# A GLA/GQA encoder on one core: weight negations ordered behind the weight casts, and the first norm sum in another part of a product

## The chip, the cores and the metric

The kernel runs on one core of a Trainium2 chip. It computes a two-layer encoder in a single launch. The metric is device time in microseconds (us). Each quoted time of a kernel is the median of several runs; the profile is one execution of its own, taken by the hardware profiler, and its time is given beside the median wherever both occur.

The core has five engines with a queue of instructions each: TensorE (PE in the profile, with its weight loads as PEld), VectorE (DVE), ScalarE (ACT), GpSimd (POOL) and SyncE (SP). Each queue is worked off in order, so an instruction that waits holds up everything behind it on its engine. Here SP does nothing but start loads from DRAM, and POOL does nothing but start accumulating transfers (a transfer whose destination is added to, not overwritten).

## The reference

The input is 512 tokens of width 1024, with 16 learned tokens put in front, so 528 columns. Each of the two layers is a feed-forward block, a mixer and another feed-forward block, all on normalised input and all added to the running state:

```python
D_MODEL, SEQ, DEPTH, N_META, D_FF = 1024, 512, 2, 16, 2816
def rmsnorm(x, g):
    return x * lax.rsqrt(jnp.mean(x * x, axis=-1, keepdims=True) + EPS) * g
def swiglu(x, w_gate, w_up, w_down):
    return (jax.nn.silu(x @ w_gate) * (x @ w_up)) @ w_down
for l in range(DEPTH):
    h = h + 0.5 * swiglu(rmsnorm(h, gain[l, 0]), w_gate[l, 0], w_up[l, 0], w_down[l, 0])
    h = h + mixer(rmsnorm(h, gain[l, 1]), ...)      # gated linear attention + grouped-query attention
    h = h + 0.5 * swiglu(rmsnorm(h, gain[l, 2]), w_gate[l, 1], w_up[l, 1], w_down[l, 1])
return rmsnorm(h, final_norm)[:, N_META:]
```

All inputs are float32. The change touches the four feed-forward blocks only.

## The kernel before

**Splitting.** Every float32 weight block of 128x1024 is split into a high and a low part: ScalarE casts it (`whi`, line 342), VectorE subtracts the cast from the block (`wlo`, line 343). Activations are split likewise. A product is then three sets of matmuls: high by high, high weight by low activation, low weight by high activation.

**Seven products in place of eight.** A feed-forward block is worked as 2x2 block products by a Strassen-like scheme with seven products. Gate and up weights go in 11 pairs (line 748), most of them by seven products of 24 matmuls each; the down product goes in 4 groups of seven products per block (function `seven`, line 867), 16 such groups in the kernel. In the steady stretch a unit consists of two pairs and one down group, 21 products. In tile names, `_00_8` means layer 0, first block, pair 8; numbers 11 to 14 stand for the four down groups, so `_00_13` is the third down group.

**Weight sums.** Five of the seven products use sums of the four blocks `w11`, `w12`, `w21`, `w22`. They are made like this: `base` loads `w21` into a sum buffer and an accumulating transfer adds `w22` to it (`base_sum`). `first_sums` (called once `w11` of the pair is on its way) makes two negated copies of `w11` on ScalarE (`negative`, line 290, names `s3` and `s2`), then has `w21` from DRAM added to `s3` and the base sum added to `s2` (`add`, line 295). `last_sum` makes a negated copy of `w12` (`s4`) and adds `s2` to it. The sums are then cast and split like any block: `whi<-s`.

**Buffers.** There are three buffers for raw blocks, four plus one each for the high and the low parts, and seven for sums. SP's loads wait for a free raw buffer, a cast waits until TensorE has done with the high part that its buffer held.

**What sets the order.** The program text is turned into queues by a scheduler that goes by priority and by dependencies: an instruction may stand ahead of others that precede it in the text when its inputs are held to be ready earlier. `with self.after(ins):` adds an order-only dependency: what stands inside comes behind `ins` on its queue. Before the change a negation has none, so the scheduler places it by its load.

**Other lines that the prediction speaks of.** The activations between gate/up and down: the partial products are copied out of PSUM (`c`, line 758) and added up on VectorE (line 763), scaled (788, 805), passed through silu on ScalarE (511), multiplied, and split into the high and low operands `g` of the down product by a cast on ScalarE (828) and a subtraction on VectorE (829). The blocks begin with pair products in another form (`first_pair`, line 703) that also needs the norm: squares, column sums by a matmul (540), `rs` (553, 511, 557), all from `norm.rs`, called inside `first_pair`.

Of the kernel before, what the change touches and what calls it, by code (L numbers as in the profile page):

```python
# [13 lines left out]
AF = mybir.ActivationFunctionType  # L14
# [58 lines left out]
def lasts(begin):  # L73
    return [2 * g + begin + 2 for g in range(SEVENS)]
# [132 lines left out]
class Groups:  # L207


    def __init__(self, tc):  # L210
        self.tc, self.layer, self.groups, self.counts = tc, 0, {}, {}
# [16 lines left out]
class Weights:  # L228
# [3 lines left out]
    def __init__(self, nc, after, raw, hi, lo, wts, win, wdn):  # L232
        self.nc, self.raw, self.hi_pool, self.lo_pool, self.wts, self.win, self.wdn = nc, raw, hi, lo, wts, win, wdn
        self.sum_pool = None
        self.loads = []
        for t, col in zip(PLAN, COLUMN):
            if t[0] == "op":
                self.loads.append(t[1:])
            elif col % SLAB == 0:
                self.loads.append(col // SLAB)  # L240
        self.at = {load: i for i, load in enumerate(self.loads)}
        self.made, self.fetched, self.got, self.summed, self.raws, self.second = 0, 0, {}, {}, {}, {}
        self.pos, self.behind, self.after = 0, None, after
        ops = [i for i, load in enumerate(self.loads) if not isinstance(load, int)]
        self.apart = set(ops[4::5])
        self.extra = None
        self.bases, self.agenda = [], []
        for i in ops:
            f, p, product = self.loads[i]
            if product == "1":  # L250
                early = p >= NPAIR or f == (0, 0) and p == 2 or p - 1 in lasts(f == (0, 0))
                at = i - LEAD * early
                self.bases.append((at, (f, p)))
                self.agenda += [(at, 0, (f, p))] + [(i, 1, (f, p))] * early
        self.bases.sort()
        self.agenda.sort()
# [30 lines left out]

    def negative(self, f, i, name, w):
        t = self.sum_pool.tile([P, SLAB], F32, tag="ws", name=f"{name}_{f[0]}{f[1]}_{i}")
        self.nc.scalar.activation(t, w, AF.Copy, scale=-1.0)  # L290
        return t

    def add(self, t, src):
# [33 lines left out]
    def make(self, upto):  # L327
        nc = self.nc
        while self.made < min(upto, len(self.loads)):
            self.fetch(self.made + 1)  # L330
            s = self.made
            load = self.loads[s]
            summed_first = not isinstance(load, int) and load[1] >= NPAIR and load[2] == "6"
            w = self.raws.pop(s, None)
            if w is None:
                w = self.summed.pop(load)
            hi = self.slab("whi", self.hi_pool, s in self.apart, f"whi{s}")
            lo = self.slab("wlo", self.lo_pool, s in self.apart, f"wlo{s}")
            for a in np.split(np.arange(SLAB), 2 if s == 0 else 1):
                cs = slice(a[0], a[-1] + 1)  # L340
                with self.after(self.behind if load == ((0, 0), 2, "6") or load in RESERVED or summed_first else None):
                    nc.scalar.copy(hi[:, cs], w[:, cs])  # L342
                nc.vector.tensor_tensor(lo[:, cs], w[:, cs], hi[:, cs].bitcast(F32), ALU.subtract)  # L343
            self.got[s] = (hi, lo)
            self.got.pop(s - 12, None)
            self.made += 1
            if not isinstance(load, int):
                if load[2] == "1" and load[:2] not in self.second:
                    self.first_sums(*load[:2], w)
                elif load[2] == "2":  # L350
                    self.last_sum(*load[:2], w)
# [39 lines left out]
def build(tc, ctx, xt, wts, win, wdn, par, w2, const, umask, out):  # L391
    nc = tc.nc
# [12 lines left out]
    def after(ins):  # L405
        return tc.issue_after(ins) if ins is not None else nullcontext()
# [36 lines left out]
    def pair(second=False):  # L443
        return (slots["s2"] if second else pss).tile([P, 2, 512], F32, tag="s2" if second else "ss", name=nm("ss"))
# [227 lines left out]
    def ffn(l, f, norm, done, following):  # L672

        x, rs, n = norm.x, None, live[0]
        w = n // 2
# [13 lines left out]
        def quarters():  # L689
            return slots["c"].tile([P, 4 * T], F32, tag="c", name=nm("c"))[:, : 4 * n].rearrange("p (j q c) -> p j q c", j=2, q=4)  # L690
# [3 lines left out]
        def first_pair(p, m):  # L694

            accs = [pair(m == "1") for _ in range(2)]
            blocks = [W.op((l, f), p, m + c) for c in "12"]
            for r, (hi, lo) in enumerate(blocks):
                for k, (first, second) in enumerate(zip(x, norm.second)):
                    for j, acc in enumerate(accs):  # L700
                        for i, (a, b) in enumerate(((hi, 0), (hi, 1), (lo, 0))):
                            for t, v in enumerate((first, second)):
                                last = TE.matmul(acc[:, t, :w], a[:, j, k], v[b][:, r], start=k == 0 and r == 0 and i == 0,  # L703
                                                 stop=k == len(x) - 1 and r == 1 and i == 2)
                    if (p, m, r, k) == (1, "2", 1, 0):
                        with after(last.ins):
                            factor.append(norm.rs("s2", urgent=False))
            st = made.setdefault(p, {})
            if "c" not in st:
                st["c"] = quarters()  # L710
            at = 2 * (m == "2")
            for j, acc in enumerate(accs):
                with tc.high_priority():
                    W.behind = S.copy(st["c"][:, j, at : at + 2], acc[:, :, :w]).ins
# [179 lines left out]
        for i, step in enumerate(steps):  # L894
            now[0] = i
            if step[0] == "P":
                product_of_pair(*step[1:])
                if step[2] == "7" and rs is None:
                    rs = norm.rs("ss" if second(step[1]) else "s2", urgent=False)
                if i == last_op:  # L900
                    close_pools(norm.pools)
                    following()
            elif step[0] == "F":
                for c in SQUARES.get(step[1:], ()):
                    norm.square(c)
                first_pair(*step[1:])
                if step[1:] == (1, "1"):
                    for j in range(KC // 2):
                        norm.pair(j)
                elif step[1]:  # L910
                    rs = factor.pop()
                    for m in range(2):
                        hidden(made[0], 0, m)
                        put_off(i + 1, lambda m=m: hidden(made[1], 1, m))
            elif step[0] == "O":
                two_products(*step[1:])
            elif step[0] == "S":
                seven(*step[1:])
            else:
                down(*step[1:])  # L920
            for fn in later.pop(i, ()):
                fn()
# [635 lines left out]
```

## Time and profile before

| | |
|---|---|
| median of three runs | 2216.25 us (2212.53 to 2220.52) |
| the profiled execution | 2211.28 us |
| its span, first to last instruction | 2209.5 us |
| TensorE busy with matmuls / weight loads | 2158.2 us (98%) / 2072.5 us (94%) |
| VectorE busy | 1719.5 us (78%) |
| ScalarE busy | 1378.2 us (62%) |
| GpSimd busy (issuing transfers) | 204.1 us (9%) |
| negations: 174 on ScalarE | 183.6 us |
| weight casts from blocks, sums and raw slabs: 241 + 174 + 126 | 252.6 + 182.8 + 132.3 us |

Profile rows name a group of instructions by line, engine, operation and tiles (`out<-in`, numbers left out), how often it occurs, its busy time, the mean duration of one in ns, and the idle time of the engine just ahead of it with what ended that idle time. Timeline rows give start and duration in us from the start of the span. The busy share of TensorE is from modelled ends of pipelined matmuls, so a wait of a few tenths of a microsecond can be hidden in it; the idle time ahead of weight loads shows more of them.

### The profile page before, as it was taken

Reading aid. Unit: us, or ns where it says so; the run is one execution under the profiler, and the core shown is the slowest. Engines: PE = TensorE matmul, PEld = TensorE weight load, DVE = VectorE, ACT = ScalarE, POOL = GpSimd, SP = SyncE. Lnnn points to the kernel's source line nnn. Section 1 sums busy time; section 2 is a strip of 40 time slices with the busy share of each in tenths; the row PEclk is TensorE's granted clock in tenths of the full one; section 3 lists DMA queues with packets and bytes.
Section 4 is the critical chain, followed back from the end, with each engine's and each line's share of the span. In section 5 each row is a group of like instructions: output and inputs, shape, how many; then the busy total and the mean of one; then the engine's idle time right before and its main releaser. Section 6 shows DMA issues by size and latency. Waiting matters only on the chain.

```text
span 2209.5 us, 40509 instructions
## 1 busy us (share of the span) xinstructions
PE 2158.2 (98%) x16572; PEld 2072.5 (94%) x16572; DVE 1719.5 (78%) x2627; ACT 1378.2 (62%) x2022; POOL 204.1 (9%) x236
## 2 busy tenths in 40 slices
PE   9999999999999999999999999999999999999998
PEld 9899999999999999999999999999888888999997
DVE  7888877577976688888688888775789867878885
ACT  8666646355784576666586666554567937666654
POOL 1111100000000011111011111000000001111100
PEclk9999999999999999999999999999999999999999
DMA  8788843211113688888488888532221238878851
GB/s 249 174 200 210 204 112 125 80 60 64 39 39 108 155 196 204 207 193 198 128 194 209 193 198 202 128 125 77 67 69 47 70 103 205 190 192 206 205 152 64
DMA packets 90746, 322.60 MB, mean 146 GB/s; under 512 B 10048, under 2 KB 12352, under 8 KB 90560
## 3 DMA queue, kind: packets, MB, share of 16 engines
q0 software_dynamic: 33408, 121.65, 30.5%
q1 hardware_dynamic: 55072, 195.13, 26.5%
q10 hardware_dynamic: 2080, 3.23, 0.4%
q8 instruction: 130, 2.13, 0.4%
q14 instruction: 56, 0.46, 0.1%
HBM read 257.06 MB, written 2.10 MB: 117 GB/s over the span
## 4 chain that ended last, share of the span: by engine, by line
PE 77%; DVE 9%; ACT 7%; DMA 5%; issue 2%; DVEq 0%; ACTq 0%; SPq 0%
PE ss L748 29%; PE ss L867 14%; PE mm L528 12%; PE ss L528 10%; DMA w<-win 5%; DVE wlo L343 3%; ACT whi L342 3%; PE ss L703 2%; PE sm L528 2%; PE sm L1237 1%; PE ss L1211 1%; ACT t L511 1%; ACT s L290 1%; PE sm L1255 1%; PE sm L1256 1%
## 5 line engine op out<-in xcount | busy, mean ns | idle before, releaser
L748 PE MATMUL ss<-xc,whi 128*128 128x264 f32 (+1 forms) x4608 | 841.6, 284 | 4.7 <-ACT c L758 4.7
L748 PEld LDWEIGHTS ss<-xc,whi 128*128 128x128 f32 x4608 | 714.6, 189 | 6.1 <-ACT c L758 5.9
L748 PE MATMUL ss<-xc,wlo 128*128 128x264 f32 (+1 forms) x2304 | 653.9, 284 | 0.0
L748 PEld LDWEIGHTS ss<-xc,wlo 128*128 128x128 f32 x2304 | 434.5, 189 | 0.0
L528 PE MATMUL mm<-x,whi 128*128 128x264 f32 (+1 forms) x1712 | 383.2, 314 | 0.0
L342 ACT CAST whi<-w 128x1024 fp32r<-128x1024 f32 (+1 forms) x241 | 252.6, 1048 | 179.3 <-PE ss L748 151.9
L867 PE MATMUL ss<-g,whi 128*128 128x264 f32 (+1 forms) x1792 | 336.5, 287 | 25.6 <-DVE g L829 13.1
L343 DVE TENSOR_TENSOR wlo<-w,whi 128x1024 fp32r<-128x1024 f32 (+1 forms) x241 | 293.5, 1218 | 84.5 <-ACT whi L342 84.1
L867 PEld LDWEIGHTS ss<-g,whi 128*128 128x128 f32 x1792 | 280.6, 190 | 31.6 <-DVE g L829 16.4
L528 PEld LDWEIGHTS mm<-x,whi 128*128 128x128 f32 x1712 | 278.3, 188 | 15.7 <-DVE x L517 0.2
L343 DVE TENSOR_TENSOR wlo<-s,whi 128x1024 fp32r<-128x1024 f32 x174 | 212.6, 1222 | 99.9 <-ACT whi L342 99.6
L342 ACT CAST whi<-s 128x1024 fp32r<-128x1024 f32 x174 | 182.8, 1051 | 131.6 <-PE ss L748 64.5
L528 PE MATMUL mm<-x,wlo 128*128 128x264 f32 (+1 forms) x856 | 264.5, 314 | 0.0
L867 PE MATMUL ss<-g,wlo 128*128 128x264 f32 (+1 forms) x896 | 255.1, 285 | 0.0
L290 ACT ACTIVATE s<-w 128x1024 f32<-128x1024 f32 x174 | 183.6, 1057 | 73.2 <-DMA w<-win 41.7
L342 ACT CAST whi<-raw 128x1024 fp32r<-128x1024 f32 x126 | 132.3, 1050 | 144.9 <-PE mm L528 69.1
L343 DVE TENSOR_TENSOR wlo<-raw,whi 128x1024 fp32r<-128x1024 f32 x126 | 154.0, 1222 | 78.8 <-ACT whi L342 78.0
L867 PEld LDWEIGHTS ss<-g,wlo 128*128 128x128 f32 x896 | 170.6, 190 | 0.0
L528 PEld LDWEIGHTS mm<-x,wlo 128*128 128x128 f32 x856 | 159.6, 188 | 7.4
L871 DVE TENSOR_TENSOR h<-h,ss 128x528 f32<-128x528 f32 (+1 forms) x224 | 154.2, 697 | 8.7 <-PE ss L867 5.3
L528 PE MATMUL ss<-g,whi 128*128 128x264 f32 (+1 forms) x764 | 142.7, 302 | 1.3 <-ACT g L516 1.3
L528 PEld LDWEIGHTS ss<-g,whi 128*128 128x128 f32 x764 | 111.6, 188 | 6.9 <-ACT g L516 1.5
(300 smaller groups left out, 3342.5 us busy)
## 6 DMA issues: line engine op xcount, KB each, us to landing
w<-win SPq DMA_DIRECT2D x175, 512.0 KB, 4.6
raw<-wts SPq DMA_DIRECT2D x126, 512.0 KB, 3.4
w<-wdn SPq DMA_DIRECT2D x64, 512.0 KB, 5.1
s<-w POOLq DMA_DIRECT2D x58, 512.0 KB, 6.2
s<-s POOLq DMA_DIRECT2D x58, 512.0 KB, 5.8
w<-win POOLq DMA_DIRECT2D x42, 512.0 KB, 8.6
s<-win POOLq DMA_DIRECT2D x42, 512.0 KB, 7.8
w<-wdn POOLq DMA_DIRECT2D x16, 512.0 KB, 7.6
```

Of the source, the lines that this page charges most:

```text
L290: self.nc.scalar.activation(t, w, AF.Copy, scale=-1.0)
L342: nc.scalar.copy(hi[:, cs], w[:, cs])
L343: nc.vector.tensor_tensor(lo[:, cs], w[:, cs], hi[:, cs].bitcast(F32), ALU.subtract)
L511: prev_act[0] = S.activation(*args, **kw).ins
L528: TE.matmul(acc.half[i][:width], lhs, rhs[:, acc.spans[i]], start=first, stop=last)
L703: last = TE.matmul(acc[:, t, :w], a[:, j, k], v[b][:, r], start=k == 0 and r == 0 and i == 0, stop=k == len(x) - 1 and r == 1 and i == 2)
L748: TE.matmul(acc[:, j], a[:, j, k], b[:, at], start=bool(begin and k == 0 and i == 0), stop=k == len(x) - 1 and i == 2, skip_group_check=no ...
L867: TE.matmul(acc[:, j], a[:, 2 * half + j, k], b, start=bool(begin and k == 0 and i == 0), stop=k == 1 and i == 2, skip_group_check=not begin)
L871: V.tensor_tensor(to, to, acc, ALU.add)
L1211: TE.matmul(s[:n, i, :HF], lhs, kh[:, hs], start=True, stop=False)
L1237: TE.transpose(tp[:, j * w + u * n : j * w + (u + 1) * n], pr[:n, (2 * c2 + j) * P : (2 * c2 + j + 1) * P], ident[:n, :n])
L1255: TE.matmul(o[:, :w], vw, ph, start=i == 0, stop=False)
```

## The change

Two things change. First, the weight cast keeps its instruction in `self.latest`, and `negative` is issued with an order-only dependency on it: each negation stands on ScalarE's queue behind the weight cast that precedes it in the text. Second, in the first block only, the column sums of the norm (`norm.rs`) are called after the step (row 0, chunk 1) of a product of pair 1 in place of (row 1, chunk 0). No arithmetic is added or left out.

```diff
@@ class Weights, __init__
-        self.extra = None
+        self.extra = self.latest = None
@@ negative
         t = self.sum_pool.tile([P, SLAB], F32, tag="ws", name=f"{name}_{f[0]}{f[1]}_{i}")
-        self.nc.scalar.activation(t, w, AF.Copy, scale=-1.0)
+        with self.after(self.latest):
+            self.nc.scalar.activation(t, w, AF.Copy, scale=-1.0)
         return t
@@ make
                 with self.after(self.behind if load == ((0, 0), 2, "6") or load in RESERVED or summed_first else None):
-                    nc.scalar.copy(hi[:, cs], w[:, cs])
+                    self.latest = nc.scalar.copy(hi[:, cs], w[:, cs]).ins
                 nc.vector.tensor_tensor(lo[:, cs], w[:, cs], hi[:, cs].bitcast(F32), ALU.subtract)
@@ first_pair
-                    if (p, m, r, k) == (1, "2", 1, 0):
+                    if (p, m, r, k) == (1, "2", 0, 1):
                         with after(last.ins):
                             factor.append(norm.rs("s2", urgent=False))
```

After the change, line numbers from 291 on are one higher (342 becomes 343, and so on). Queues before and after are quoted below by row; a row has the line, the operation and the tiles with their numbers.

ScalarE's queue where the third down group of the first block begins (`c119` is the gate/up activation of that group, `g132` to `g137` its split operands, `whi65` the cast of the sum `s2` of group 13, `s3_00_8` and `s2_00_8` the negations for pair 8), before:

```order
L342 CAST whi64_2611<-s4_00_7_2350 128x1024
L511 ACTIVATE c119_2256<-c119_2256 128x528
L290 ACTIVATE s3_00_8_2783<-w11_00_8_2756 128x1024
L342 CAST whi65_2646<-s2_00_13_2505 128x1024
L828 CAST g132_2604<-c119_2256 128x528
L290 ACTIVATE s2_00_8_2785<-w11_00_8_2756 128x1024
L758 COPY c130_2438<-ss129_2407 128x2x264
L828 CAST g135_2641<-c119_2256 128x528
```

The same place with the change:

```order
L343 CAST whi64_2611<-s4_00_7_2350 128x1024
L512 ACTIVATE c119_2256<-c119_2256 128x528
L343 CAST whi65_2646<-s2_00_13_2505 128x1024
L829 CAST g132_2604<-c119_2256 128x528
L343 CAST whi66_2683<-w12_00_13_2615 128x1024
L759 COPY c130_2438<-ss129_2407 128x2x264
L829 CAST g135_2641<-c119_2256 128x528
L291 ACTIVATE s4_00_13_2687<-w12_00_13_2615 128x1024
L343 CAST whi67_2721<-s3_00_13_2503 128x1024
L829 CAST g137_2676<-c119_2256 128x528
L845 ACTIVATE g139_2680<-c119_2256 128x264
L343 CAST whi68_2752<-w21_00_13_2412 128x1024
```

The two negations of pair 8 no longer stand between the silu and `g135`; they follow behind `whi68`. The negation `s4` of group 13, which stood in front of `whi61`, now follows `g135`.

ScalarE's queue a little earlier, where the negated copy `s2` of group 13 is made (the sum that `whi65` casts), with the change:

```order
L759 COPY c119_2256<-ss118_2226 128x2x264
L291 ACTIVATE s3_00_13_2503<-w11_00_13_2476 128x1024
L291 ACTIVATE s2_00_13_2505<-w11_00_13_2476 128x1024
L343 CAST whi61_2509<-s3_00_7_2268 128x1024
L343 CAST whi62_2543<-w11_00_13_2476 128x1024
```

Before, `s2_00_13` stood two casts further up, in front of `whi59`, and `s3_00_13` one cast above that; both now stand directly in front of `whi61`, one behind the other, and GpSimd starts their transfers in the same order as before.

ScalarE's queue in the first block, around the copy `c63` of the first product of pair 3, before:

```order
L342 CAST whi13_839<-s3_00_2_341 128x1024
L516 CAST t58_776<-c21_319 128x528
L511 ACTIVATE c34_576<-c34_576 128x528
L342 CAST whi14_875<-w12_00_3_798 128x1024
L516 CAST t60_783<-c21_319 128x528
L511 ACTIVATE c34_576<-c34_576 128x528
L290 ACTIVATE s3_00_11_1039<-w11_00_11_1012 128x1024
L758 COPY c63_824<-ss62_787 128x2x264
```

With the change:

```order
L343 CAST whi12_788<-w11_00_3_651 128x1024
L715 COPY c34_576<-ss52_644 128x528
L517 CAST t60_783<-c21_319 128x528
L291 ACTIVATE s3_00_3_792<-w11_00_3_651 128x1024
L291 ACTIVATE s2_00_3_794<-w11_00_3_651 128x1024
L759 COPY c63_824<-ss62_787 128x2x264
L512 ACTIVATE c34_576<-c34_576 128x528 x2
L343 CAST whi13_839<-s3_00_2_341 128x1024
```

The copy `c63` now comes before `whi13`; it stood behind `whi13`, `whi14`, the silus and the negation `s3` of group 11. In their place the two negations of pair 3 stand in front of it. The norm's chain (553, 511, 557), which stood between `whi11` and `whi12`, stands between `whi10` and `whi11` with the change.

## The prediction

> **What bounds the kernel now.** I read the page's busy times and chain first, then the waits of TensorE, then the timelines of the engines around one such wait.
>
> ```profile
> PE 2158.2 (98%) x16572; PEld 2072.5 (94%) x16572; DVE 1719.5 (78%) x2627; ACT 1378.2 (62%) x2022; POOL 204.1 (9%) x236
> PE 77%; DVE 9%; ACT 7%; DMA 5%; issue 2%; DVEq 0%; ACTq 0%; SPq 0%
> ```
>
> ```profile
> 300.00:420.00 120.00, 120.00 (x986) 119.71 (x985) 73.21 (x96) 54.70 (x74) 0.00 (x0) 1.00 0.31 99
> ```
>
> TensorE is the bound by sheer work, and where it has its operands (the 120 us from 300 to 420, the second row) it is busy without a gap at granted clock 1.00. So the number of matmuls sets a floor that the change does not touch, and only gaps of TensorE can be won or added. Yet 23% of the chain is not TensorE: each such piece is a place where it had to wait. The waits tell where.
>
> ```profile
> PE ss L867 <- DVE g L829: 13.1, 16, 0.8
> PE ss L867 <- ACT g L828: 12.5, 10, 3.2
> PE ss L748 <- ACT c L758: 4.7, 5, 3.0
> ```
>
> ```profile
> L867 PEld LDWEIGHTS ss<-g,whi 128*128 128x128 f32 x1792 | 280.6, 190 | 31.6 <-DVE g L829 16.4 <-ACT g L828 15.2
> ```
>
> The first two rows are one event each time: the start of a down group, waiting for its first operands `g`, the high part from ScalarE and the low part from VectorE. There are 16 down groups and 16 waits of the second kind, none above 0.8 us; 10 of the groups have the ScalarE wait on top. By the matmuls' modelled ends that is 25.6 us; by the weight loads (last row), which carry no modelled end, 31.6 us, or 1.98 us a group. I take 31.6.
>
> One of the 16, the third group of the first block, on TensorE, ScalarE, VectorE:
>
> ```profile
> 221.57 0.51 PE L867 MATMUL ss<-g,whi 128*128 128x264 f32 x2 [0.31 <-ACT g L828]
> 222.91 0.39 PE L867 MATMUL ss<-g,whi 128*128 128x264 f32 x1 [0.84 <-DVE g L829]
> ```
>
> ```profile
> 214.57 1.05 ACT L342 CAST whi<-s 128x1024 fp32r<-128x1024 f32 x1 [1.37 <-PE ss L748]
> 216.72 0.65 ACT L511 ACTIVATE c<-c 128x528 f32<-128x528 f32 x1 [1.10 <-DVE c L788]
> 218.99 1.06 ACT L290 ACTIVATE s<-w 128x1024 f32<-128x1024 f32 x1 [1.62 <-DMA w<-win]
> 219.95 1.03 ACT L342 CAST whi<-s 128x1024 fp32r<-128x1024 f32 x1
> 220.89 0.63 ACT L828 CAST g<-c 128x528 fp32r<-128x528 f32 x1
> ```
>
> ```profile
> 218.48 0.71 DVE L834 TENSOR_TENSOR c<-c 128x528 f32<-128x528 f32 x1
> 221.01 1.23 DVE L343 TENSOR_TENSOR wlo<-s,whi 128x1024 fp32r<-128x1024 f32 x1 [1.36 <-ACT whi L342]
> 222.16 0.70 DVE L829 TENSOR_TENSOR g<-c,g 128x528 fp32r<-128x528 f32 x1
> ```
>
> ```profile
> 213.98 4.92 DMA w<-win
> ```
>
> ScalarE is free at 217.37, after the silu. Next in its queue stands a negation for pair 8, work for a product still far off, and its `w11` was only issued at 213.98 and lands at 218.90 (last row, from the chain of waits). So ScalarE stands 1.62 us, negates for 1.06, casts `whi65`, and only then the high operand `g132` that TensorE wants; VectorE has `wlo65` ahead of the low operand in its queue, so the delay passes on to it. This is the wait behind a load, summed over the kernel:
>
> ```profile
> ACT s L290 <- DMA w<-win: 41.7, 18, 5.7
> ```
>
> **The change, part by part.**
>
> *1. Negations behind the casts (the main term).* The queue now runs silu, `whi65`, `g132`. When could `whi65` start? It needs a buffer that TensorE gives back once per product; `whi64` got its one at 214.57, a product takes 24 matmuls of about 0.122 us, 2.92 us, so 217.49. Then `whi65` ends near 218.5, `g132` runs to about 219.1. TensorE would reach that operand, without the 0.31 us, at about 221.1: on time by two. On VectorE `wlo65` can start at 219.2, when the L834 instruction ends, takes 1.23, then `g133` ends at about 221.1; TensorE wants it two matmuls after the high part, 221.3. So both waits fit, the second with only 0.2 us over. I keep 0.2 us a group, 3.2 in all (0 to 0.5 a group are the bounds: VectorE may have one more short instruction of 0.43 in front). Term: -31.6 + 3.2 = **-28.4**.
>
> *2. The sums come later.* The negation of group 13's `s2` stood here:
>
> ```profile
> 199.38 1.06 ACT L290 ACTIVATE s<-w 128x1024 f32<-128x1024 f32 x1 [1.29 <-DVE wlo L343]
> 203.84 0.59 ACT L758 COPY c<-ss 128x528 f32<-128x528 f32 x1
> ```
>
> ```profile
> 200.84 0.88 POOL L295 DMA_DIRECT2D s<-w  x1 [6.35 <-ACT s L290]
> 207.75 0.87 POOL L295 DMA_DIRECT2D s<-s  x1 [6.03 <-DMA s<-w]
> ```
>
> Its transfer was issued on GpSimd at 200.84. Now `s3` and `s2` both follow the copy at 203.84: 204.4 to 206.5, and the transfers start at about 205.5 and 206.6. The second must have landed at 217.5 to leave `whi65` where part 1 puts it: 10.9 us. What these transfers took:
>
> ```profile
> s<-w POOLq DMA_DIRECT2D x1, 512.0 KB, 6.3
> ```
>
> ```profile
> 761.22 1.24 POOL L295 DMA_DIRECT2D s<-win  x1
> 763.28 0.87 POOL L295 DMA_DIRECT2D s<-w  x1 [0.82 <-ACT t L601]
> ```
>
> ```profile
> s<-win POOLq DMA_DIRECT2D x1, 512.0 KB, 10.7
> s<-w POOLq DMA_DIRECT2D x1, 512.0 KB, 12.4
> ```
>
> ```profile
> s<-w POOLq DMA_DIRECT2D x58, 512.0 KB, 6.2
> ```
>
> The first is this one, 6.3 us between 200 and 214; the next are a pair issued 2 us apart, at 761.22 and 763.28, and each took about twice as long. The last row is the median of all 58. Now they go out a microsecond apart in all groups, so the price lies between 6.2 (0 late) and 12.4 (1.5 late). I take 8 to 10, no delay, since SP's loads here are few; with 12.4 it would cost up to 1.5 us a group, and since `whi65` stood at 219.95 before, even that leaves something of the gain. The base of pair 8 (`w21`) is now loaded behind its `w11` and its addition stands on GpSimd behind `s4` of group 13, whose negation now comes at about 225 (the transfer started at 207.75 before).
>
> ```profile
> 233.81 1.05 ACT L342 CAST whi<-w 128x1024 fp32r<-128x1024 f32 x1 [0.38 <-PE ss L867]
> 242.62 1.06 ACT L342 CAST whi<-s 128x1024 fp32r<-128x1024 f32 x1 [0.93 <-PE ss L867]
> ```
>
> These are the casts of `w11` and `s2` of pair 8. The sum lands near 241 for a cast at 242.62: tight, but a cast is made some four products, 11 us, before TensorE uses it, so a late sum there delays only the short copies behind it. For such new waits I add **+1.5**, bounds 0 and 9 (the 42 gate/up sums, each a fifth of a microsecond).
>
> Raw blocks: `w11` is held until its negations are done, now a little after its own cast; 2 x 1.06 us later, with SP's next load not due for several microseconds. Nothing on ScalarE is added: 174 negations stay 174.
>
> *3. The norm in the first block.*
>
> ```profile
> 52.62 0.65 ACT L557 ACTIVATE t<-rs 128x528 f32<-128x528 f32 x1
> 53.81 1.06 ACT L342 CAST whi<-w 128x1024 fp32r<-128x1024 f32 x1
> ...
> 62.73 0.64 ACT L511 ACTIVATE c<-c 128x528 f32<-128x528 f32 x1
> 64.38 1.06 ACT L290 ACTIVATE s<-w 128x1024 f32<-128x1024 f32 x1 [1.01 <-ACT c L511]
> 65.34 0.58 ACT L758 COPY c<-ss 128x528 f32<-128x528 f32 x1
> ```
>
> ```profile
> 62.62 0.40 PE L748 MATMUL ss<-xc,whi 128*128 128x264 f32 x2
> 65.98 0.81 PE L748 MATMUL ss<-xc,whi 128*128 128x264 f32 x2 [2.96 <-ACT c L758]
> ```
>
> TensorE stands 2.96 us until the copy `c63` has emptied the PSUM tile that the next product adds to. That copy waits behind the silus, which need `rs`, and a negation. With the change `rs`, whose last step on ScalarE is the row at 52.62, is there some 4.4 us sooner (the call is three steps earlier in its product, each 12 matmuls of 0.122 us), and the copy stands ahead of the silus, behind the two negations of pair 3, which can be over at about 59: `whi12` was cast at 53.81, and a copy, a cast of 0.64 and two negations follow it, 4 us with gaps of a few tenths. Without the wait TensorE would want it at about 63, when the matmul before it starts. I keep 0.5: **-2.5** (bounds -2.96 and 0).
>
> *4. Other copies.* The remaining 1.7 us of that row (4.7 in 5 waits, less 2.96) are four copies at the beginnings of the other blocks, each behind a negation. Some of these negations move away: **-0.9** (bounds -1.7 and 0).
>
> Sum: -28.4 + 1.5 - 2.5 - 0.9 = **-30.3**. The profiled execution took 2211.28 us (span 2209.5), which gives 2181.0; it lies 5 us below the median of the three runs, 2216.25, and just below their lowest. On the median it is **2186**, which I predict.
>
> **The rivals.**
>
> *A. The sums are late, and the kernel gets slower.* One mechanism: transfers in pairs land so late that `whi65` waits for `s2` at the head of ScalarE's queue, with `g132` behind it. It decides once `whi65` would start after 219.95, that is, from a landing time of 219.95 - 206.6 = 13.3 us. For it: the 12.4 us pair, one microsecond short; 1.13 us more between the two issues there than here. Against: the median of 6.2. Each microsecond beyond costs 16 us; at 15.5 us, +2.2 x 16 = +35, so 2251. The Trainium skill ("DMA: Bandwidth & Descriptors", section "Issuing engines are not separate DMA queues") says that transfers from all issuing engines run on the same 16 DMA engines and interleave, which speaks for a collision with SP's loads. The trace agrees in the 10.7 and 12.4 us rows; by that rule alone 12.4 would be the figure, and the gain up to 24 us smaller.
>
> *B. VectorE takes over.* `g132` is early but the low operand stays behind `wlo65` and other VectorE work, or the sums are late within the bound. Then the 13.1 us of waits for L829 stay, and of 31.6 only 15.2 to 18.5 go. With -2.5 and -0.9 and some +3 for late sums: -15 to -18, about 2200. For it: every one of the 16 groups shows that wait, whatever ScalarE did, and my margin is 0.2 us. Against: in the rows above VectorE idles 1.36 us for `whi65` just before.
>
> *C. The wait is one of buffers and only moves.* The load of `w11` was issued at 213.98 because a raw block came free then; if late blocks set the pace, a cast instead of a negation will wait for it. Then nothing is won: within 3 us of 2216, so 2213 to 2216. Against: the block of pair 8 is cast 14 us later than it landed, at 233.81. The Trainium skill ("Perfetto Trace Analysis", "Identifying Performance Opportunities") says that the same bubble repeated on the saturated engine can mean that memory for the next tile ran out. The bubble repeats 16 times here, but the rows show ScalarE free and an operand's source ready, so the trace bears this out little.
>
> *D. Only the first block gains*, if ScalarE's order in the 16 groups were not what was in the way: -2.5, 2213.
>
> **How the numbers follow.** The forecast has 0.62, B 0.20, C and D together 0.11, A 0.07. The forecast's own range is 2174 (36.3 us, all waits of parts 1, 3 and 4, go, and the base is about 2211) to 2197 (residual of 0.5 a group, 8 us, and 9 us for sums). The range that should hold the time 8 times in 10 reaches over B: 2173 to 2207. A measurement of this kernel can tell about 0.3%, 6.6 us, from no change. Forecast and B lie below 2209.6: faster 0.82. C and D are within: same 0.11. A: slower 0.07.
>
> **What would show it.** In the profile of the changed kernel: the L867 rows of TensorE's waits shrink from 25.6 us to under 4 and the weight-load row from 31.6 to under 6 (1); the row for negations waiting for `w<-win` shrinks from 41.7 to a few microseconds, and the chain no longer passes from that load to L290 (1); no long wait of a cast for a sum (`whi` for the transfer `s<-w`) in front of `g` (2, A); the wait at 65.98 under 1 us (3). If the ScalarE wait is gone and the VectorE wait of about 0.8 stays in 16 groups, B was right; if casts wait for `w<-win` by as much, C. The forecast is wrong if the span is above 2198 or below 2172.

## The result

| | before | with the change |
|---|---|---|
| median | 2215.03 us (2212.53 to 2220.52) | **2181.90 us** (2179.88 to 2182.74) |
| span of the profiled execution | 2209.5 us | 2180.6 us |
| idle ahead of the down groups' weight loads (867 / 868) | 31.6 us | 0.0 us |
| idle ahead of the gate/up products' weight loads (748 / 749) | 6.1 us | 14.6 us |
| casts waiting for a sum's transfer `s<-w` | none listed | 102.8 us, 29 times |

The change makes the kernel faster: the ratio is 0.9846, with a 95% interval of 0.9825 to 0.9866, 33 us at the medians (28.9 us between the two profiled spans). The forecast was 2186 and its range 2173 to 2207.

The page of the changed kernel, busy times and chain:

```profile
PE 2148.4 (99%) x16572; PEld 2067.0 (95%) x16572; DVE 1712.3 (79%) x2627; ACT 1369.9 (63%) x2022; POOL 204.1 (9%) x236
...
PE 81%; DVE 6%; ACT 5%; DMA 4%; issue 3%; POOL 0%; SPq 0%; DVEq 0%; ACTq 0%; POOLq 0%
PE ss L749 32%; PE ss L868 14%; PE mm L529 14%; PE ss L529 11%; DMA s<-w 3%; PE sm L529 2%; DVE wlo L344 1%; DMA w<-win 1%; ACT whi L343 1%; PE sm L1238 1%; PE ss L1212 1%; ACT t L512 1%; PE sm L1256 1%; PE sm L1257 1%; PE ss L1213 1%
```

TensorE's share of the chain rises from 77% to 81%. The loads of weights from DRAM (`w<-win`) fall in the chain from 5% to 1%, and L290/291, the negation, is no longer listed; a new entry is the sums' transfer, `DMA s<-w`, at 3%.

Two groups before, the weight loads of the gate/up products and the casts of sums:

```profile
L748 PEld LDWEIGHTS ss<-xc,whi 128*128 128x128 f32 x4608 | 714.6, 189 | 6.1 <-ACT c L758 5.9
L342 ACT CAST whi<-s 128x1024 fp32r<-128x1024 f32 x174 | 182.8, 1051 | 131.6 <-PE ss L748 64.5 <-PE ss L867 59.8 <-issue 4.2
```

With the change, the groups of weight loads, of casts of sums and of negations:

```profile
L749 PEld LDWEIGHTS ss<-xc,whi 128*128 128x128 f32 x4608 | 713.9, 189 | 14.6 <-ACT c L759 11.3 <-DVE c L764 3.0
L868 PEld LDWEIGHTS ss<-g,whi 128*128 128x128 f32 x1792 | 277.0, 188 | 0.0
L343 ACT CAST whi<-s 128x1024 fp32r<-128x1024 f32 x174 | 180.9, 1047 | 182.5 <-DMA s<-w 102.8 <-PE ss L749 43.9 <-PE ss L868 28.5
L291 ACT ACTIVATE s<-w 128x1024 f32<-128x1024 f32 x174 | 179.9, 1055 | 9.7 <-DMA s<-s 9.7
```

The second row is the main term, gone altogether. The last row: negations waited 41.7 us for `w<-win`; now none do. The first and third rows show what came in exchange. The same down group as in the prediction, on ScalarE, VectorE and TensorE:

```profile
211.99 0.65 ACT L512 ACTIVATE c<-c 128x528 f32<-128x528 f32 x1 [1.05 <-DVE c L789]
212.81 1.05 ACT L343 CAST whi<-s 128x1024 fp32r<-128x1024 f32 x1 [0.17 <-PE ss L749]
213.77 0.63 ACT L829 CAST g<-c 128x528 fp32r<-128x528 f32 x1
```

```profile
214.37 1.22 DVE L344 TENSOR_TENSOR wlo<-s,whi 128x1024 fp32r<-128x1024 f32 x1
215.51 0.70 DVE L830 TENSOR_TENSOR g<-c,g 128x528 fp32r<-128x528 f32 x1
```

```profile
216.36 0.41 PE L868 MATMUL ss<-g,whi 128*128 128x264 f32 x2
216.60 0.28 PE L868 MATMUL ss<-g,wlo 128*128 128x264 f32 x1
```

The cast `whi65` follows the silu by 0.17 us, the high operand is there at 214.40, two microseconds ahead of the matmuls at 216.36 that want it. The low operand ends at 216.21, one or two tenths of a microsecond ahead of its use. The cover on VectorE is as thin as reckoned, but in this kernel it holds in all 16 groups; with the negations alone (first experiment) one group waits 0.7 us there.

### The profile page after: what moved, and what is told of

Read it like the earlier page. It is cut to its first block, busy times and chain, and to the rows that moved or that the text cites. A ratio compares the mean times of both kernels' runs of the same rounds, so it can differ in the third digit from the quotient of the medians.

```text
span 2180.6 us, 40542 instructions
## 1 busy us (share of the span) xinstructions
PE 2148.4 (99%) x16572; PEld 2067.0 (95%) x16572; DVE 1712.3 (79%) x2627; ACT 1369.9 (63%) x2022; POOL 204.1 (9%) x236
## 4 chain that ended last, share of the span: by engine, by line
PE 81%; DVE 6%; ACT 5%; DMA 4%; issue 3%; POOL 0%; SPq 0%; DVEq 0%; ACTq 0%; POOLq 0%
PE ss L749 32%; PE ss L868 14%; PE mm L529 14%; PE ss L529 11%; DMA s<-w 3%; PE sm L529 2%; DVE wlo L344 1%; DMA w<-win 1%; ACT whi L343 1%; PE sm L1238 1%; PE ss L1212 1%; ACT t L512 1%; PE sm L1256 1%; PE sm L1257 1%; PE ss L1213 1%
## 5 line engine op out<-in xcount | busy, mean ns | idle before, releaser
L749 PEld LDWEIGHTS ss<-xc,whi 128*128 128x128 f32 x4608 | 713.9, 189 | 14.6 <-ACT c L759 11.3
L868 PE MATMUL ss<-g,whi 128*128 128x264 f32 (+1 forms) x1792 | 327.0, 283 | 0.0
L343 ACT CAST whi<-s 128x1024 fp32r<-128x1024 f32 x174 | 180.9, 1047 | 182.5 <-DMA s<-w 102.8
L868 PEld LDWEIGHTS ss<-g,whi 128*128 128x128 f32 x1792 | 277.0, 188 | 0.0
L868 PE MATMUL ss<-g,wlo 128*128 128x264 f32 (+1 forms) x896 | 253.9, 283 | 0.0
L868 PEld LDWEIGHTS ss<-g,wlo 128*128 128x128 f32 x896 | 168.7, 188 | 0.0
L529 PE MATMUL ss<-g,whi 128*128 128x264 f32 (+1 forms) x764 | 142.8, 302 | 1.3 <-ACT g L517 1.3
```

The costliest lines, as they stand in the source:

```text
L343: self.latest = nc.scalar.copy(hi[:, cs], w[:, cs]).ins
L529: TE.matmul(acc.half[i][:width], lhs, rhs[:, acc.spans[i]], start=first, stop=last)
L749: TE.matmul(acc[:, j], a[:, j, k], b[:, at], start=bool(begin and k == 0 and i == 0), stop=k == len(x) - 1 and i == 2, skip_group_check=no ...
L868: TE.matmul(acc[:, j], a[:, 2 * half + j, k], b, start=bool(begin and k == 0 and i == 0), stop=k == 1 and i == 2, skip_group_check=not begin)
```

## The experiments

All kernels below ran beside the kernel before on the same chip; ratios are to it.

**1. The two parts apart.** One kernel has only the ordered negations (the `r, k` test put back to `1, 0`), the other only the norm's move.

> The change without its second part: negations behind the casts, the norm's column sums where they were. Theory (the gain is the 16 down groups' wait): L868 rows of TensorE's waits stay at 0, the first block's wait for the copy c63 comes back in part (0 to 3 us, with up to 1.2 us of slow matmuls behind it), so 0 to 4 us above the full change, 2182 to 2186. Rival (the norm's move does a third or more of it, since it starts the first block earlier and shifts all that follows): 2192 or more.

> The change without its first part: only the norm's column sums move. Theory: the 31.6 us ahead of L867's weight loads stay as they are; the wait of 2.96 us at 66 us and the slow matmuls behind it (1.2 us) go, a new wait at the column sums (1.6 us in the full change at 45.8) comes: 1 to 4 us below before, 2211 to 2214. Rival (the norm's move does a third or more): 2204 or less.

Negations alone: 2180.41 us (2179.16 to 2181.41), ratio 0.9847 (0.9830 to 0.9864), a little below what its theory had. Norm alone: 2214.17 us, ratio 0.9995 (0.9981 to 1.0009). The whole gain is in the negations; the norm's move gives nothing that can be measured, a little less than its theory had. Why shows in the waits of TensorE with the norm's move alone, and in the row at its column sums:

```profile
PE ss L540 <- ACT t L534: 3.6, 1, 3.6
```

```profile
49.25 0.81 PE L540 MATMUL ss<-t,whole 128*128 128x264 f32 x2 [3.58 <-ACT t L534]
```

The wait of 2.96 us at 65.98 is gone, but not because its copy comes sooner: the first copy of line 758 starts at 66.99 here, against 65.34 before. TensorE comes there later, because the column sums, put earlier into the product, now wait 3.58 us for their operand. In the kernel with the negations alone there is no wait at 66 us either, and there the copy does come sooner: it starts at 61.35, ahead of the two casts and the negation behind which it stood before (two other negations, of pair 3, now precede it). A wait of 1.4 us for a copy comes at 75.7 us instead.

**2. The late sums.** What is left, 14.6 us ahead of the gate/up products, was put down to sums. At the beginning of the last block, with the change, on ScalarE and TensorE:

```profile
1866.77 1.05 ACT L343 CAST whi<-s 128x1024 fp32r<-128x1024 f32 x1 [5.55 <-DMA s<-w]
1867.72 0.63 ACT L512 ACTIVATE c<-c 128x512 f32<-128x512 f32 x1
1868.26 1.03 ACT L343 CAST whi<-s 128x1024 fp32r<-128x1024 f32 x1
1869.71 0.62 ACT L829 CAST g<-c 128x512 fp32r<-128x512 f32 x1 [0.43 <-DVE c L806]
1870.24 1.04 ACT L343 CAST whi<-w 128x1024 fp32r<-128x1024 f32 x1
1871.18 0.58 ACT L759 COPY c<-ss 128x512 f32<-128x512 f32 x1
```

```profile
1871.82 0.51 PE L749 MATMUL ss<-xc,whi 128*128 128x256 f32 x2 [2.77 <-ACT c L759]
```

A cast stands 5.55 us for the transfer of its `s2`; a silu, two more casts and the copy (759) pile up behind it; the matmul that wants the PSUM tile emptied by that copy waits 2.77 us. If that is the cause, the sums concerned must come earlier. They are those of pairs whose `first_sums` is called right after their own cast of `w11`; with the change their negations stand behind that cast. The next kernel leaves these alone free:

```diff
-    def first_sums(self, f, i, w):
-        s3, s2 = [self.negative(f, i, n, w) for n in ("s3", "s2")]
+    def first_sums(self, f, i, w, ordered=True):
+        s3, s2 = [self.negative(f, i, n, w, ordered) for n in ("s3", "s2")]
@@ negative
-        with self.after(self.latest):
+        with self.after(self.latest if ordered else None):
@@ make
-                    self.first_sums(*load[:2], w)
+                    self.first_sums(*load[:2], w, ordered=False)
```

> The full change, but the negations s3 and s2 of the pairs whose sums are formed only after their own cast of w11 are free again (as before the change); those of the pairs and groups formed ahead of it, and all s4, stay ordered. Theory (the 14.6 us that are left ahead of L749's weight loads come from casts that stand at the head of ScalarE's queue for a late sum): casts' wait for the transfer s<-w falls from 102.8 us to under 35, the L749 wait from 14.6 to under 5, L868 stays at 0: 2170 to 2175. Rival one (those waits come from where the copies now stand, not from the sums): within 2 us of 2182. Rival two (freed negations return to the place in front of g): L868 waits come back, 2190 or more.

2172.65 us (2170.78 to 2174.68), ratio 0.9813 (0.9795 to 0.9830): 9 us below the change. Its groups:

```profile
L749 PEld LDWEIGHTS ss<-xc,whi 128*128 128x128 f32 x4608 | 712.6, 188 | 3.0 <-ACT c L759 2.1 <-DVE c L764 0.6
L868 PEld LDWEIGHTS ss<-g,whi 128*128 128x128 f32 x1792 | 277.1, 188 | 0.0
L343 ACT CAST whi<-s 128x1024 fp32r<-128x1024 f32 x174 | 181.8, 1048 | 149.4 <-DMA s<-w 54.5 <-PE ss L749 46.5 <-PE ss L868 40.8
```

The gate/up wait falls to 3.0 us and the time falls with it, as the theory had it: the late sums were the cause. At the beginning of the last block TensorE now works without a wait. Casts still wait 54.5 us for sums, more than the 35 expected, and that costs TensorE next to nothing: what counts is a wait at the head of the queue with something urgent behind it. With the norm's sums put back as well:

> The kernel with free negations for the pairs formed after their own cast (2172.65 us), and the norm's column sums back where they were before the change. Theory (the norm's move only exchanges a wait of some 3 us at 66 us for one of some 3 us ahead of the column sums): the wait at L541 (2.94 us at 47.8) goes, and no other of more than 1 us comes at 60 to 80 us: 2168 to 2172. Rival (the move was needed for this order too): a wait for the copy c63 of 2 to 3 us is back, 2172 to 2176.

2169.93 us (2168.85 to 2171.14), ratio 0.9810 (0.9789 to 0.9831). All its runs lie below all runs of the change, and it is the fastest kernel of this study. Against the kernel above, 2172.65, it is 2.7 us lower at the medians; the two ranges overlap, so that step is not settled. One wait of 1.59 us for the copy came at 63.9, between the theory (none over 1 us) and the rival (2 to 3 us).

**3. Which negation must be ordered?** Only `s4`, with all `s3` and `s2` free; then `s4` free and the others ordered.

> The full change, but only s4 is ordered; all s3 and s2 are free. In the queue the spot in front of g132 is clear all the same (s3 of pair 8 now stands behind g135), s2 of the down group stands where it did before. Theory (what counts is what stands between the last silu and g, whichever negation was ordered): L868 near 0 in most groups and the sums on time, 2168 to 2185. Rival (s3 and s2 themselves must be ordered, since their load is what is waited for): half or more of the 31.6 us are back, 2197 or more.

> The full change with s4 alone free, s3 and s2 ordered. Theory (it is s3 and s2 of the next pair that stood in front of g; s4 stood elsewhere): L868 waits near 0, 2176 to 2190. Rival (s4 must be ordered with them): 2197 or more.

`s4` alone: **2250.52 us**, ratio 1.0164 (1.0142 to 1.0186), slower than before. Neither the theory nor the rival holds: the time lies where the rival put it, but the waits in front of `g` are 0, as the theory has it, and a new one comes which neither named. Its waits of TensorE and ScalarE, and one place on ScalarE:

```profile
PE ss L749 <- ACT c L759: 53.2, 13, 6.5
```

```profile
ACT s L291 <- DMA s<-s: 66.9, 15, 6.0
```

```profile
199.97 1.05 ACT L343 CAST whi<-s 128x1024 fp32r<-128x1024 f32 x1 [2.20 <-DMA s<-w]
206.68 1.06 ACT L291 ACTIVATE s<-w 128x1024 f32<-128x1024 f32 x1 [5.66 <-DMA s<-s]
207.65 0.58 ACT L759 COPY c<-ss 128x528 f32<-128x528 f32 x1
```

The free `s2` of the down group stands as far up as before the change, and waits 5.66 us for a transfer that reads a sum and adds it to another, with the copy behind it. My reading: its sum buffer is still read by the transfer that adds `s2` of pair 7 to `s4` of pair 7, and that `s4` is now ordered, so late. The profile does not name the buffer. With `s4` free and the rest ordered the time is 2191.56 us, ratio 0.9911 (0.9884 to 0.9937), a little above the theory's 2176 to 2190: `L868 <- DVE g L830` is back with 8.2 us in 10 places. Most of the gain is there, not all.

If the freed `s2` of the down groups is the culprit, then freeing it in the fast kernel must slow that one too. And if only the negations ahead of `g` mattered, ordering those alone should be enough. Three kernels from the fast one (2169.93): all `s4` free; the down groups' `s3`, `s2` free; both.

> As the kernel with free negations for the later pairs and the norm's column sums where they were, and also all negations s4 free. Theory (order matters only for what stands in front of g, and s4 is cast late enough): L868 waits stay at 0 and the time within 4 us of that kernel. Rival (s4 returns to places ahead of other casts and holds up ScalarE for its load or a sum buffer, as the free s2 did in the kernel with s4 alone ordered): 2185 or more, with a wait of L291 for a transfer of over 30 us.

> The fastest kernel so far (free negations for the later pairs, the norm where it was, 2169.93 us), with s3 and s2 of the down groups free as well. In the queue s2 of group 13 returns to its place in front of whi59, where it stands in the kernel with s4 alone ordered (2250.52 us). Theory (there s2 of a down group stands ahead of the moment at which its sum buffer comes free, since the ordered s4 of the pair before, which still reads that buffer, is late): once more a wait of L291 for the transfer s<-s of 40 us or more in some 12 places, and 2215 to 2255. Rival (it was the freed s3 and s2 of the pairs that made that kernel slow): 2168 to 2180.

> As the kernel before, with all s4 free too, so that only s3 and s2 of the pairs formed ahead of their cast are ordered: the negations that stood in front of g. Theory: s4 is early enough to give back the sum buffers (no wait of L291 for s<-s above 10 us), L868 stays near 0, but as in the kernel with free s4 (2232.60 us) a negation waits for its block (w<-win, some 80 us) in front of the other g: 2215 to 2240. Rival (order is needed for those negations alone): 2170 to 2185.

| | median | ratio | TensorE's main wait (749) | the negations' main wait (291) |
|---|---|---|---|---|
| `s4` free | 2232.60 us | 1.0089 (1.0068 to 1.0111) | 30.0 us for `g` | 83.6 us for `w<-win` |
| down groups' `s3`, `s2` free | 2239.27 us | 1.0107 (1.0076 to 1.0138) | 48.8 us for the copy `c` | 65.9 us for `s<-s` |
| both | 2236.36 us | 1.0094 (1.0062 to 1.0127) | 33.0 us for `g` | 88.0 us for `w<-win` |

The second and the third row came as their theories have it. The first went against its theory, the way its rival had it: free `s4`s leave the place ahead of the one `g` clear but go to another. On ScalarE, with `s4` free:

```profile
178.26 1.06 ACT L291 ACTIVATE s<-w 128x1024 f32<-128x1024 f32 x1 [4.59 <-DMA w<-win]
179.22 1.03 ACT L343 CAST whi<-w 128x1024 fp32r<-128x1024 f32 x1
180.16 1.06 ACT L291 ACTIVATE s<-w 128x1024 f32<-128x1024 f32 x1
181.12 1.03 ACT L343 CAST whi<-s 128x1024 fp32r<-128x1024 f32 x1
182.78 0.63 ACT L829 CAST g<-c 128x528 fp32r<-128x528 f32 x1 [0.63 <-DVE c L806]
```

A negation waits 4.59 us for its block while the other half's `g` stands behind it, and a gate/up matmul waits 2.11 us until that `g` is done, at 183.50: the same fault, at another place. So in the fast kernel neither the `s4` nor the down groups' `s3` and `s2` can be freed without losing the whole gain; to free only the pairs' `s3` and `s2` that are still ordered there was not tried. What a selection costs depends on the rest: freeing `s4` costs 10 us from the full change and 63 us from the fast kernel, and the runs do not show why. Of the five other selections, four were slower than no order at all.

**4. What a wait costs beyond itself.** In one kernel the first cast of `g` in the 16 down groups is written one to sixteen times over.

```diff
-                S.copy(hi, src)
+                for _ in range(times):        # 1, 2, ... 16, one more in each group
+                    S.copy(hi, src)
```

> The full change, with the first cast of g in each of the 16 down groups written 1, 2, ... 16 times over (0.63 us each, the same result): group n gets n - 1 extra. It shows the slack that the change has left at this place, and what a wait costs beyond itself. Theory (a wait of TensorE of over some 3 us is followed by some 14 matmuls at 0.22 us in place of 0.12, 1.2 to 1.5 us more): up to the slack no wait, then waits that grow by about 0.6 us a group, and slow matmuls behind those of over 2 to 3 us only. Rival one (the slow matmuls come from elsewhere, such as the transfers): they stand behind short waits as often. Rival two (no slack, as reckoned ahead of the change: 0.2 us): waits from the second group on.

2257.76 us, one run. The scheduler spread the copies between the casts and put some of them early, so the slack of the change cannot be read from it cleanly: groups 1 to 8 show no wait above 0.6 us at the weight loads, the ninth one of 2.6 us for a weight cast, the last seven waits for `g` of 3.9 to 8.4 us, growing by 0.5 to 1.3 us. What stands behind such a wait does show, in group 12:

```profile
1390.19 1.33 PE L871 MATMUL ss<-g,whi 128*128 128x264 f32 x4 [4.89 <-ACT g L830]
1391.32 0.42 PE L871 MATMUL ss<-g,wlo 128*128 128x264 f32 x1
...
1394.21 0.28 PE L871 MATMUL ss<-g,wlo 128*128 128x264 f32 x1
```

A matmul takes 0.42 us right behind the wait and 0.28 us some 4 us after it. All seven of those waits have such a tail. Whether short waits have one as often, as the first rival has it, is counted in the last section.

## Why the prediction was right, and where it was not

The time was right, and its main mechanism too. But one term was mis-sized by some ten microseconds and one was missing, and that they offset each other is luck.

- *Term 1, negations behind the casts: forecast -28.4.* Measured -31.6 at the weight loads. The walk through the queues held: `whi65` right behind the silu, the low operand just in time. The residual of 0.2 us a group was not there.
- *Term 2, the sums come later: forecast +1.5, bounds 0 and 9.* This term was mis-sized. The waits ahead of the gate/up products rose from 6.1 to 14.6 us. The experiment with free later negations takes away 11.6 of the 14.6, so by that run the late sums cost 11.6 us there, above the upper bound; the net of 8.5 is smaller because some 3 us of the old waits on that row went. The prediction had looked at `s2` of the down group and of pair 8, both formed ahead of their own cast: these indeed came in time (`whi65` waits 0.17 us and the cast of pair 8's `s2`, now at 236.28, 0.94 us, both for a buffer and not for a sum). It said that a late sum "delays only the short copies behind it". But TensorE waits for these copies, as at 1871.82; the next product adds to the PSUM tile that they empty.
- *Terms 3 and 4, the first block and the other copies: forecast -2.5 and -0.9.* The wait at 66 us went, but in the kernel with the norm's move alone only because TensorE waited earlier instead: the move brought its own wait at the column sums (3.58 us alone, 0.96 in the full change). By the run of the norm alone this part is worth nothing.
- *The term that was missing.* After some waits TensorE runs at half pace (the last section has the granted clock). Counted from the starts of weight loads, four waits before were followed by such a tail (66, 828, 1908 and 1971 us, 5.3 us in all), with the change one (808 us, 1.5 us): -3.9 us.

From the rows: -31.6 + 8.5 - 3.9 makes -27.0 of the 28.9 us between the spans; the remaining 1.9 us were not traced to a place. The sum of the prediction was -30.3.

Rival A (sums late enough to be slower) did not come about at its place, ahead of `g`: the median of the 58 transfers `s<-w` of the profile's page rose from 6.2 to 7.8 us, not to 12.4. Late sums as such were real, and cost about 9 us at another place (2181.90 against 2172.65). Rival B is refuted: VectorE idled before because ScalarE was late, and the low operand came in time. Rival C is refuted: no negation waits for `w<-win` now, and casts wait for it 7.3 us in place of 4.7, so they did not take over the 41.7. Rival D is refuted, and the reverse holds: it is the norm's move that gives nothing by itself.

## What to carry to other kernels

When an engine with an in-order queue waits for a load, look at what stands behind that instruction, and move the waiting one behind work whose inputs are sure; but its own consumers then come later, so put it no further back than they bear. Here ordering all negations won 33 us, ordering all but those formed after their own cast won 43, and five other selections lost part or all of it: with shared buffers and one queue the places hang together, and a selection has to be tried as a whole. A wait that is large on an engine off the path (54.5 us for sums in a fast kernel) says nothing until one sees who is queued behind it.

## What the runs showed of the hardware

A TensorE wait can cost more than its length. In the kernel before, the largest wait, and the granted clock in two windows behind it (columns: busy time of PE, PEld, DVE, ACT, POOL, granted clock, share of the transfers, GB/s):

```profile
1907.76 0.50 PE L867 MATMUL ss<-g,whi 128*128 128x256 f32 x2 [3.21 <-ACT g L828]
```

```profile
1909.10:1912.00 2.90, 2.89 (x13) 2.90 (x14) 2.17 (x4) 2.04 (x4) 0.84 (x1) 0.50 1.02 194
1913.00:1916.00 3.00, 3.00 (x28) 3.00 (x27) 3.00 (x5) 1.53 (x3) 0.00 (x0) 1.00 0.32 64
```

For about 3 us behind the wait the clock granted is 0.50, and 13 matmuls start in 2.90 us where 28 start in 3.00 us later. Counted over the feed-forward products' weight loads in all twelve profiles (a wait is the gap between two starts less 0.122 us; a tail is 8 or more of the next 35 starts at 0.17 to 0.25 us apart; a wait stands alone when no other above 0.3 us lies within 28 weight loads of it):

| wait | cases | with a slow tail | alone | of these with a tail |
|---|---|---|---|---|
| 1.0 to 1.5 us | 56 | 10 | 24 | 0 |
| 1.5 to 2.0 us | 16 | 5 | 4 | 0 |
| 2.0 to 3.0 us | 31 | 19 | 25 | 15 |
| 3.0 to 3.5 us | 13 | 10 | 10 | 8 |
| over 3.5 us | 31 | 31 | 24 | 24 |

So no wait below 2 us that stood alone had a tail, which refutes the first rival of the fourth experiment. A tail costs 1.1 to 2.6 us more. The Trainium skill ("TensorE: Matmul & The Clock Gate", section "Why this matters for your kernels") says that idle gaps of over about 3 us between bursts of matmuls bring the clock back to half. The runs agree above 3.5 us, where every wait has a tail; between 2 and 3 us more than half of the waits have one, earlier than that rule has it.
